# A two-layer backbone block on one core: layer 1's merge with tokens on the partitions, and one adaLN projection moved from TensorE to VectorE

## The chip, the core and the metric

The program runs on one core of one Trainium2 chip. The metric is the device time in microseconds of one execution. The engines are called as the profile calls them: PE is TensorE's matmul side and PEld its weight load, DVE is VectorE, ACT is ScalarE, POOL is GpSimd, SP is SyncE, which here issues the DMAs.

## The reference

Two layers over 256 latent tokens and 256 context tokens of 1024 channels. Each layer mixes tokens in three parallel branches (windowed attention A, global attention B, a bidirectional gated linear recurrence C), merges them with sigmoid gates, projects, and runs a squared-ReLU MLP. The shift, scale and gate rows of both halves come from adaLN projections of a conditioning vector. Layer 1 needs the latent stream alone in the merge, the output projection and the MLP.

```python
def _merge(ya, yb, yc, g, w_br_a, w_br_b, w_br_c, w_out):
    ga, gb, gc = jnp.split(jax.nn.sigmoid(g), N_BRANCH, axis=-1)
    return (ga * (ya @ w_br_a) + gb * (yb @ w_br_b) + gc * (yc @ w_br_c)) @ w_out
...
for l in range(DEPTH):
    with_ctx = l < DEPTH - 1
    mod_lat = (jax.nn.silu(c) @ w_ada[l] + b_ada[l])[:, None, :]
    mod_ctx = (jax.nn.silu(c_ctx) @ w_ada[l] + b_ada[l])[None, None, :]
    sh1, sc1, g1, sh2, sc2, g2 = jnp.split(mod_lat, 6, axis=-1)
    ...
    o_lat, o_ctx = _token_mixer(x * (1.0 + sc1) + sh1, ctx * (1.0 + csc1) + csh1, ...)
    x = _layernorm(ALPHA * x + g1 * o_lat, ln1_g[l], ln1_b[l])
    x = _layernorm(ALPHA * x + g2 * _sq_relu_mlp(x * (1.0 + sc2) + sh2, w_ff1[l], w_ff2[l]),
                   ln2_g[l], ln2_b[l])
```

## The kernel before

**Products.** Every float32 matrix is split into a rounded high part and the rest, and a product is three matmuls: high by high, high by rest, rest by high. The weights come in units of 1 MB (512 KB for the branch matrices of A and B), one DMA each into one of three `raw` buffers. ACT rounds a unit in four pieces into `whi` (`split`, L120), DVE subtracts for `wlo` (L128); in the recurrence stage every second piece of `whi` is DVE's too (L122). `take` hands out the next unit, and `prefetch` behind it issues the next loads and queues the next unit's pieces; `tick`, called between matmuls, emits them.

**Two forms of product.** `cm` keeps 128 channels of a weight unit stationary and moves the tokens: 512 columns in layer 0, 256 in layer 1, result with channels on the partitions (`ps_cm`). `tm` and `unit` keep 128 tokens stationary and move 256 or 512 weight columns, result with tokens on the partitions (`ps_tm`).

**Stages.** In each layer: recurrence (`lru`, with the key and value projections, and in layer 1 the first queries), attention interleaved by `pair` with a filler, which holds the other queries, the merge gates (`merge_gates`) and the branch products (`merge_branch`); then output projection (`wout`), residual, LayerNorm and transposes into channels (`tail_units`, `ln_t`, `ln_h`), MLP. In the span of the profiled execution layer 1's recurrence runs from about 940 to 1145 us, attention with the merge from 1100 to 1284, the output projection to 1306, the MLP to the end.

**Layer 1's merge.** The twelve gate units and the twelve branch units go through `cm` with 256 columns: 3 x 4 x 2 x 8 x 3 = 576 matmuls for the gates, 2 x 4 x 2 x 4 x 3 + 4 x 2 x 8 x 3 = 384 for the branches, 960 in all. ACT takes the tanh of each 128x256 gate block out of PSUM, DVE multiplies it with the branch block (L1163) and adds it up (L1168), and the sum's blocks, channels on the partitions, are split for the output projection.

**adaLN projections.** Beside the first one, each projection covers 2048 columns in eight steps of 128 rows. `ada_queue` plans them, `ada_step`, called from `prefetch`, starts the next step when the planner's PE time has passed `ada_at`: it first emits what is left of the step before, then the step's 1 MB load into a `raw` buffer. With `dve` set a step is eight DVE instructions that multiply and add 128x512 (L293, the first step L291), emitted one at a time by `tick` over the pace `ADA_PACE`, and PE adds the partitions up once at the end; without it a step is four 512-column matmuls on PE. The planner's time runs on its own costs (0.42 ns a column). While steps are queued, `prefetch` loads weights two units ahead, else three:

```python
self.emit_dma(i + 3 if not self.ada_q else i + 2)
```

**Order.** The framework orders each engine's instructions when the kernel is built; an engine then runs them strictly in that order, so a DVE instruction that waits holds back all DVE instructions behind it, and with them the `wlo` pieces that PE needs next.

Of the kernel before, what the change touches and what calls it, by code (L numbers as in the profile page):

```python
# [9 lines left out]
F32R = mybir.dt.float32r  # L10
AF = mybir.ActivationFunctionType
# [36 lines left out]
class Kern:  # L48
# [95 lines left out]
    def plan_units(self):  # L144
# [9 lines left out]
        for l in range(DEPTH):  # L154
            win = a["w_in"][l]
            order = ("xr0 yr0 xr1 yr1 xr2 yr2 xr3 yr3 kvA qA0 kvB qA1 qB0 qB1",
                     "xr0 xr1 yr0 yr1 kvA xr2 yr2 kvB xr3 yr3 qA0 qA1 qB0 qB1")[l]
            for n in order.split():
                key = (n,) if n[:2] == "kv" else (n[:2], int(n[2]))
                U.append(((l,) + key, cols(win, COL[key[0]] + 256 * sum(key[1:])), KD))  # L160
            for what, br in self.MERGE[l]:
                for n in range(4):
                    if what == "g":
                        U.append(((l, "g", br, n), cols(win, COL["g"] + 1024 * "abc".index(br) + 256 * n), KD))
                    else:
                        k = KD if br == "c" else KD // 2
                        U.append(((l, "br", br, n), cols(a["w_br_" + br][l], 256 * n, 0, k), k))
            for n in range(2):
                U += [((l, "wo", n, h), wide(a["w_out"][l], 512 * n, 512 * h), KD) for h in range(2)]
            f1 = [((l, "f1", n // 4, n % 4), cols(a["w_ff1"][l], 256 * n), KD) for n in range(16)]  # L170
            f2 = [((l, "f2", q, n, h), wide(a["w_ff2"][l], 512 * n, 1024 * q + 512 * h), KD)
                  for q in range(4) for n in range(2) for h in range(2)]
            for q in range(4):
                U += f1[4 * q + (q > 0):4 * q + 5] + f2[4 * q:4 * q + 4]
# [13 lines left out]
            self.u_dma += 1  # L188

    def is_wide(self, i):  # L190
        return self.units[i][0][1] in ("wo", "f2")

    def shaped(self, t, i):

# [128 lines left out]
            else:  # L323
                self.ada_q.append((lambda k=k: dma(k), [], lambda k=k: mms(k), 0.0))

    ADA_PACE = (9500, 18000)

    ADA = (('bra0',0,4,1),('bra0',0,8,1),('mlp0',1,0,1),('mlp0',1,4,1),('ga1',1,8,0))

    def ada_start(self, at):  # L330
        for a, l, b, dve in self.ADA:
# [792 lines left out]
    def merge_gates(self, l, br):  # L1124
# [1 line left out]
        cols = BOTH if l == 0 else LAT  # L1126
        self.tg[br] = []
        for n in range(4):
            w = self.take((l, "g", br, n))
            if br == "c":  # L1130
                if n == 1:
                    while any(step[2] for step in self.bg):
# [5 lines left out]
                elif n > 1:  # L1138
# [3 lines left out]
                        self.y["C"].append((hi, lo))  # L1142
                    if n == 3:
                        self.flags.add((l, "y", "C"))
            for b, t in enumerate(self.g2(l, "tg")):
                yield from self.cm(w, self.h, cols, b)
                self.act(t[:, cols], self.out, AF.Tanh, scale=0.5)
                self.tg[br].append(t)

    def merge_branch(self, l, br, first, last):  # L1150
        nc = self.nc
# [1 line left out]
        k = KD if br == "c" else KD // 2  # L1153
        while (l, "y", br.upper()) not in self.flags:
            yield "need"
        ys = self.y.pop(br.upper())
        for n in range(4):
            w = self.take((l, "br", br, n))
# [131 lines left out]
    def tail_units(self, l, which, keys, xs):  # L1290
# [6 lines left out]
            self.hn = [(self.g("h_hi", F32R), self.g("h_lo", F32R)) for _ in range(KD)]  # L1297
        if l:
            ws = []
            for tb, j in ((2, 0), (2, 1), (3, 0), (3, 1)):  # L1300
                if tb == 2:
                    ws.append(self.take(keys[j]))
                self.unit(keys[j], ws[j], xs, (tb,), True)
# [46 lines left out]
    def wout(self, l):  # L1350
        self.start_residual(l, 1)
        if l == 0:
            self.load_x(l)
        for h in range(2):
            self.unit((l, "wo", 0, h), self.take((l, "wo", 0, h)), self.m_hl(), self.tbs, True)
        self.tail_units(l, 1, [(l, "wo", 1, 0), (l, "wo", 1, 1)], self.m_hl())
        self.m = {}

# [112 lines left out]
    def layer(self, l):  # L1471
        a = self.a
        self.ada_start("layer%d" % l)
        self.layer_consts(l)
        self.ks, self.qs, self.qt, self.vv, self.y, self.m, self.tg, self.qs_at = {}, {}, {}, {}, {}, {}, {}, {}
        self.lru(l)
        if l == 0:
# [122 lines left out]
```

## Time and profile before

| | |
|---|---|
| median of three timed runs | 1508.69 us (1506.35 to 1509.06) |
| the profiled execution | 1507.38 us, its span 1505.6 us |
| busy, share of the span | PE 97%, PEld 81%, DVE 77%, ACT 51%, POOL 19% |
| mean granted TensorE clock | 0.989 |
| matmuls | 8364 records |

The page's shares are means over very different stages; the windows of the trace give them for a stretch, the chain of waits tells what ended last, and the timeline of an engine shows each instruction with the idle time before it and what ended that. A matmul's own duration overlaps its neighbours', so a matmul is priced by a row of many divided by their number, and a DVE instruction from its start to the next one's start.

### The profile page before, as it was taken

What the parts mean: (1) busy time and instruction counts of PE and PEld (TensorE: products, weight loads), DVE (VectorE), ACT (ScalarE), POOL (GpSimd) and SP (SyncE); (2) the same over time, 40 slices, a digit from 0 to 9 for tenths busy, and PEclk for the clock granted to TensorE, in tenths of its full rate; (3) what the DMA queues carried; (4) which work ended last, traced back from release to release, by engine and by line L of the source; (5) the groups of instructions that cost most, each with busy time, mean ns of one, the idle gap of its engine ahead of it and who ended that gap; (6) DMA issues with size and microseconds to landing.
All of it is one profiled execution on the core that took longest, in us unless ns stands there. A gap on an engine that the chain in (4) does not pass through costs nothing.

```text
span 1505.6 us, 22308 instructions
## 1 busy us (share of the span) xinstructions
PE 1455.2 (97%) x8364; PEld 1226.5 (81%) x8364; DVE 1154.4 (77%) x2179; ACT 772.2 (51%) x1594; POOL 292.7 (19%) x298
## 2 busy tenths in 40 slices
PE   7899999999999999899999999999899999899997
PEld 4688988777878879678878887897787899799986
DVE  4699987758688966977657768888989577886666
ACT  2698667565223327313323234587777655655452
POOL 0533422100000002711110301264411003031110
PEclk9999999999999999999999999999999999999999
DMA  9523310105557552444435343342345735755563
GB/s 325 194 85 111 113 57 29 43 29 172 169 190 247 198 198 95 159 160 159 162 112 192 116 168 110 107 143 74 123 144 178 243 109 185 251 169 186 181 193 112
DMA packets 156748, 225.69 MB, mean 150 GB/s; under 512 B 5840, under 2 KB 118992, under 8 KB 151520
## 3 DMA queue, kind: packets, MB, share of 16 engines
q1 hardware_dynamic: 156640, 224.27, 45.2%
q8 instruction: 65, 1.06, 0.3%
q14 instruction: 43, 0.35, 0.1%
HBM read 218.97 MB, written 5.28 MB: 149 GB/s over the span
## 4 chain that ended last, share of the span: by engine, by line
PE 80%; DVE 12%; ACT 4%; issue 2%; DMA 1%; POOL 0%; SPq 0%; DVEq 0%; ACTq 0%
PE ps_cm L92 42%; PE ps_tm L92 26%; DVE wlo L128 3%; PE ps_s L92 2%; PE ps_pv L92 2%; PE ps_pT L99 2%; PE ps_ada L92 2%; PE ps_gate L92 2%; DVE ada_acc L293 1%; DVE xc L647 1%; DMA raw_ada<-in_w_ada_dram 1%; PE ps_qT L99 1%; ACT L103 1%; DVE lru_q L718 1%; DVE lru_i L708 0%
## 5 line engine op out<-in xcount | busy, mean ns | idle before, releaser
L120 ACT CAST whi<-raw 128x512 fp32r<-128x512 f32 x521 | 300.1, 622 | 374.0 <-PE ps_tm L92 195.3
L128 DVE TENSOR_TENSOR wlo<-raw,whi 128x512 fp32r<-128x512 f32 x560 | 407.0, 753 | 103.2 <-ACT whi L120 98.0
L92 PE MATMUL ps_cm<-h_hi,wlo 128*128 128x256 f32 (+1 forms) x1216 | 406.9, 337 | 7.0 <-DVE wlo L128 6.9
L92 PE MATMUL ps_cm<-h_hi,whi 128*128 128x256 f32 (+1 forms) x1216 | 408.5, 340 | 3.0 <-ACT whi L120 2.0
L92 PE MATMUL ps_cm<-h_lo,whi 128*128 128x256 f32 (+1 forms) x1216 | 406.1, 336 | 0.2 <-POOL h_lo L1249 0.2
L92 PEld LDWEIGHTS ps_cm<-h_hi,whi 128*128 128x128 f32 x1216 | 230.4, 191 | 39.9 <-ACT whi L120 7.1
L92 PEld LDWEIGHTS ps_cm<-h_hi,wlo 128*128 128x128 f32 x1216 | 231.9, 191 | 34.3 <-DVE wlo L128 9.2
L92 PEld LDWEIGHTS ps_cm<-h_lo,whi 128*128 128x128 f32 x1216 | 232.0, 191 | 24.1 <-POOL h_lo L1249 0.7
L293 DVE SCALAR_TENSOR_TENSOR ada_acc<-raw_ada,silu,ada_acc 128x512 f32<-128x512 f32 x224 | 168.7, 799 | 49.6 <-DMA raw_ada<-in_w_ada_dram 49.4
L92 PE MATMUL ps_tm<-wlo,f_hi 128*128 128x512 f32 x384 | 150.2, 392 | 2.1 <-DVE wlo L128 2.1
L92 PE MATMUL ps_tm<-whi,f_hi 128*128 128x512 f32 x384 | 149.7, 390 | 0.0
L92 PE MATMUL ps_tm<-whi,f_lo 128*128 128x512 f32 x384 | 149.3, 389 | 0.0
L1188 POOL TENSOR_TENSOR x<-x,res 128x512 f32<-128x512 f32 x36 | 51.9, 1445 | 306.8 <-DVE res L1187 306.8
L92 PE MATMUL ps_tm<-wlo,h_hi 128*128 128x256 f32 x320 | 92.0, 287 | 6.1 <-DVE wlo L128 6.0
L92 PE MATMUL ps_tm<-whi,h_hi 128*128 128x256 f32 x320 | 92.9, 290 | 1.2 <-ACT lru_r L103 0.6
L92 PE MATMUL ps_tm<-whi,h_lo 128*128 128x256 f32 x320 | 91.4, 286 | 0.0
L92 PEld LDWEIGHTS ps_tm<-wlo,f_hi 128*128 128x128 f32 x384 | 72.1, 188 | 19.6 <-DVE wlo L128 5.2
L92 PEld LDWEIGHTS ps_tm<-whi,f_hi 128*128 128x128 f32 x384 | 72.1, 188 | 15.7 <-ACT whi L120 0.8
L103 ACT ACTIVATE p<-ps_s,mx 128x512 f32<-128x512 f32 (+1 forms) x96 | 58.5, 618 | 51.2 <-DVE mx L1001 29.9
L92 PEld LDWEIGHTS ps_tm<-whi,f_lo 128*128 128x128 f32 x384 | 72.1, 188 | 14.8
L685 POOL TENSOR_TENSOR lru_i<-lru_i,xc 128x512 f32<-128x512 f32 x32 | 52.8, 1680 | 89.3 <-ACT lru_i L103 89.3
L92 PEld LDWEIGHTS ps_tm<-wlo,h_hi 128*128 128x128 f32 x320 | 62.0, 194 | 7.7 <-DVE wlo L128 7.3
(173 smaller groups left out, 2449.5 us busy)
## 6 DMA issues: line engine op xcount, KB each, us to landing
raw<-in_w_ff_dram SPq DMA_DIRECT2D x64, 1024.0 KB, 5.5
raw<-in_w_in_dram SPq DMA_DIRECT2D x50, 1024.0 KB, 5.1
raw_ada<-in_w_ada_dram SPq DMA_DIRECT2D x40, 1024.0 KB, 5.0
w_ada<-in_w_ada_dram SPq DMA_DIRECT2D x32, 256.0 KB, 5.6
raw<-in_w_br_c_dram SPq DMA_DIRECT2D x8, 1024.0 KB, 5.7
raw<-in_w_out_dram SPq DMA_DIRECT2D x8, 1024.0 KB, 5.0
gw_raw<-in_v_gate_dram SPq DMA_DIRECT2D x16, 256.0 KB, 5.3
raw<-in_w_br_a_dram SPq DMA_DIRECT2D x8, 512.0 KB, 3.5
```

Of the source, the lines that this page charges most:

```text
L92: self.nc.tensor.matmul(out, lhsT, rhs, start=start, stop=stop, **kw)
L99: self.nc.tensor.transpose(out, in_, self.ident if n == 128 else self.ident[0:n, 0:n])
L103: ins = self.nc.scalar.activation(out, in_, func, **kw).ins
L120: self.nc.scalar.copy(out, in_)
L128: return self.nc.vector.tensor_tensor(lo, src, hi.bitcast(F32), op=ALU.subtract)
L293: self.nc.vector.scalar_tensor_tensor(acc, w, c, acc, op0=ALU.mult, op1=ALU.add)
L647: nc.vector.scalar_tensor_tensor(o, r3[:, :, lo_ + d:lo_ + d + n], w(j), o, op0=ALU.mult, op1=ALU.add)
L685: nc.gpsimd.tensor_tensor(ig, ig, self.xc[k[0]][0], op=ALU.mult)
L718: nc.vector.tensor_tensor_scan(h[:, cs][:, ::-1], r[:, cs][:, ::-1], ig[:, cs][:, ::-1], init, op0=ALU.mult, op1=ALU.add)
L1188: (nc.vector if last else nc.gpsimd).tensor_tensor(x, x, t, op=ALU.add)
```

## The change

Four edits.

1. **Weight units of layer 1's merge.** Gates and branches are loaded as 512 rows by 512 columns: four units for each gate (column half `n`, row half `h`), two each for branches A and B, four for C, so that every unit is 1 MB and one load.
2. **Tokens on the partitions.** `tw` computes them with 128 tokens stationary and 512 weight columns moving, for the two token blocks, over two units where the rows need two; two PSUM tiles stay open in between. It is 480 matmuls of 512 columns. Tanh, product and sum are taken at 128x512: 12, 12 and 8 instructions in place of 24, 24 and 16. `merge_t` transposes the sum back into channels on PE, 2 x 8 transposes of 128x128, and splits it; the first half stands inside the last branch unit, the second inside the first unit of the output projection, which for this is taken token block by token block.
3. **Order of the last two units of layer 1's output projection**: both token blocks on the first unit, then both on the second (before: both units on the first block, then on the second).
4. **The third projection of layer 1** (`sc2`, `g2`): from PE steps started at the first gate of layer 1 to DVE steps queued behind the two others at the start of layer 0's MLP; the pace of layer 1's projections goes from 18000 to 10500.

```diff
             for what, br in self.MERGE[l]:
+                if l:
+                    for n in range(2):
+                        for h in range(2 if what == "g" or br == "c" else 1):
+                            if what == "g":
+                                src = wide(win, COL["g"] + 1024 * "abc".index(br) + 512 * n, 512 * h)
+                            else:
+                                src = wide(a["w_br_" + br][l], 512 * n, 512 * h)
+                            U.append(((l, what, br, n, h), src, KD))
+                    continue
...
-    ADA_PACE = (9500, 18000)
+    ADA_PACE = (9500, 10500)
 
-    ADA = (('bra0',0,4,1),('bra0',0,8,1),('mlp0',1,0,1),('mlp0',1,4,1),('ga1',1,8,0))
+    ADA = (('bra0',0,4,1),('bra0',0,8,1),('mlp0',1,0,1),('mlp0',1,4,1),('mlp0',1,8,1))
...
+    def tw(self, w, xs, tb, h, n_h, po):
+        whi, wlo = w
+        if h == 0:
+            po[tb] = self.ps("ps_tw")
+        o, ts = po[tb], slice(128 * tb, 128 * tb + 128)
+        for i in range(4):
+            xhi, xlo = xs[4 * h + i]
+            self.mm(o, xhi[:, ts], whi[:, i, :], h == 0 and i == 0, False)
+            self.mm(o, xhi[:, ts], wlo[:, i, :], False, False)
+            self.mm(o, xlo[:, ts], whi[:, i, :], False, h == n_h - 1 and i == 3)
+            self.tick()
+            yield
...
+    def merge_t(self, n):
+        for j in range(2):
+            p = self.ps("ps_m")
+            for b in range(2):
+                for tb in range(2):
+                    c = 128 * (2 * j + b)
+                    self.tp(p[:, 256 * b + 128 * tb:256 * b + 128 * tb + 128], self.m[2 * n + tb][:, c:c + 128])
+            hi, lo = self.g("m_hl", F32R), self.g("m_hl", F32R)
+            self.split(hi, lo, p)
...
-            for tb, j in ((2, 0), (2, 1), (3, 0), (3, 1)):
+            for tb, j in ((2, 0), (2, 1), (3, 0), (3, 1)) if final else ((2, 0), (3, 0), (2, 1), (3, 1)):
```

**Where the projection's steps come to stand: SP's queue at the end of layer 0's MLP.** `raw_ada` is the load of one step, `raw` that of a weight unit (`w_ff` the MLP's, `w_in` those of layer 1's recurrence), `b_ada` the bias load that goes with the eighth step of a projection. Before:

```order
L276 DMA raw_ada<-in_w_ada_dram 128x2048
L186 DMA raw<-in_w_ff_dram 128x4x512 x2
L276 DMA raw_ada<-in_w_ada_dram 128x2048
L186 DMA raw<-in_w_in_dram 128x8x256 x2
L285 DMA b_ada<-in_b_ada_dram 32x512 x4
L186 DMA raw<-in_w_in_dram 128x8x256 x2
L406 DMA gd<-gate_rows 2x512 x2
L1270 DMA xd<-x 128x512 x4
L186 DMA raw<-in_w_in_dram 128x8x256
L628 DMA gw_raw<-in_v_gate_dram 128x512 x2
```

After:

```order
L287 DMA raw_ada<-in_w_ada_dram 128x2048
L196 DMA raw<-in_w_ff_dram 128x4x512 x2
L296 DMA b_ada<-in_b_ada_dram 32x512 x4
L287 DMA raw_ada<-in_w_ada_dram 128x2048
L196 DMA raw<-in_w_in_dram 128x8x256
L417 DMA gd<-gate_rows 2x512 x2
L287 DMA raw_ada<-in_w_ada_dram 128x2048
L196 DMA raw<-in_w_in_dram 128x8x256 x2
L287 DMA raw_ada<-in_w_ada_dram 128x2048
L196 DMA raw<-in_w_in_dram 128x8x256
L1344 DMA xd<-x 128x512 x4
L196 DMA raw<-in_w_in_dram 128x8x256
```

Before, the last step's load of the second projection stands directly ahead of the loads of layer 1's first units, and nothing of the third is there. After, the second projection ends one step earlier, and the third one's eight loads begin behind the last unit of layer 0's MLP and stand among the loads of layer 1's recurrence, the eighth 27 rows further on.

**What DVE then has in front of it: its order around the first scan of layer 1's recurrence.** `lru_q` and `lru_i` are the recurrence's, `wlo` the pieces of the units that PE takes next, `ada_acc` the projection. Before:

```order
L122 CAST whi<-raw 128x512
L128 TENSOR_TENSOR wlo<-raw,whi 128x512 x4
L122 CAST whi<-raw 128x512 x2
L700 SCALAR_TENSOR_TENSOR lru_q<-lru_q,lru_th 128x512
L128 TENSOR_TENSOR wlo<-raw,whi 128x512 x3
L700 SCALAR_TENSOR_TENSOR lru_q<-lru_q,lru_th 128x512 x3
L128 TENSOR_TENSOR wlo<-raw,whi 128x512
L708 TENSOR_TENSOR lru_i<-lru_i,lru_q 128x512 x4
L715 SCALAR_TENSOR_TENSOR lru_q<-lru_r,lru_i 128x512
```

After:

```order
L304 SCALAR_TENSOR_TENSOR ada_acc<-raw_ada,silu,ada_acc 128x512 x5
L128 TENSOR_TENSOR wlo<-raw,whi 128x512 x3
L304 SCALAR_TENSOR_TENSOR ada_acc<-raw_ada,silu,ada_acc 128x512
L128 TENSOR_TENSOR wlo<-raw,whi 128x512
L304 SCALAR_TENSOR_TENSOR ada_acc<-raw_ada,silu,ada_acc 128x512
L122 CAST whi<-raw 128x512 x2
L304 SCALAR_TENSOR_TENSOR ada_acc<-raw_ada,silu,ada_acc 128x512
L711 SCALAR_TENSOR_TENSOR lru_q<-lru_q,lru_th 128x512
L128 TENSOR_TENSOR wlo<-raw,whi 128x512 x3
L711 SCALAR_TENSOR_TENSOR lru_q<-lru_q,lru_th 128x512 x3
L128 TENSOR_TENSOR wlo<-raw,whi 128x512
L304 SCALAR_TENSOR_TENSOR ada_acc<-raw_ada,silu,ada_acc 128x512 x3
```

Eleven multiply-adds of the projection stand where there was none; five of them come ahead of the `wlo` pieces of the next unit. All 64 of the third projection are found on DVE between the residual of layer 0's last unit and the third batch of layer 1's recurrence: 16 ahead of layer 1, 8 before the first scaled tokens are split, 16 around the first batch, 16 around the second, 8 in the third.

**The end of layer 1's merge on PE.** `ps_cm` (before) and `ps_tw` (after) are the last branch's products, `ps_tm` the output projection, `ps_m` the new transposes. Before:

```order
L92 MATMUL ps_cm<-y_hl,wlo 128x256
L92 MATMUL ps_cm<-y_hl,whi 128x256 x2
L92 MATMUL ps_cm<-y_hl,wlo 128x256
L92 MATMUL ps_tm<-whi,m_hl 128x512
L92 MATMUL ps_tm<-wlo,m_hl 128x512
L92 MATMUL ps_tm<-whi,m_hl 128x512 x2
L92 MATMUL ps_tm<-wlo,m_hl 128x512
```

After:

```order
L92 MATMUL ps_tw<-whi,y_hl 128x512 x2
L92 MATMUL ps_tw<-wlo,y_hl 128x512
L92 MATMUL ps_tw<-whi,y_hl 128x512
L99 MATMUL ps_m<-ident,tg 128x128 x8
L92 MATMUL ps_tw<-whi,y_hl 128x512
L92 MATMUL ps_tw<-wlo,y_hl 128x512
L92 MATMUL ps_tw<-whi,y_hl 128x512 x2
```

The eight transposes of the first half stand between the two token blocks of the last branch unit; the other eight follow in the same way behind the first twelve matmuls of the output projection.

## Rows read from the trace of the kernel before

**Rows 1.** The page, part 1: busy time by engine, share of the span, instructions.

```profile
PE 1455.2 (97%) x8364; PEld 1226.5 (81%) x8364; DVE 1154.4 (77%) x2179; ACT 772.2 (51%) x1594; POOL 292.7 (19%) x298
```

**Rows 2.** Windows: length; PE, PEld, DVE, ACT, POOL busy (count); PEclk; DMA share; GB/s.

```profile
600.00:660.00 60.00, 55.60 (x239) 43.46 (x238) 54.25 (x65) 18.18 (x34) 27.39 (x17) 1.00 0.51 170
870.00:940.00 70.00, 70.00 (x325) 56.41 (x323) 48.79 (x84) 27.09 (x53) 6.44 (x8) 1.00 0.39 130
...
966.00:1000.00 34.00, 32.41 (x241) 30.84 (x241) 30.32 (x53) 28.88 (x55) 12.05 (x9) 1.00 0.42 140
1050.00:1100.00 50.00, 41.93 (x276) 37.56 (x275) 45.98 (x77) 34.54 (x63) 21.43 (x27) 0.97 0.36 116
1150.00:1200.00 50.00, 50.00 (x401) 41.76 (x401) 34.00 (x77) 32.10 (x76) 6.88 (x9) 1.00 0.75 246
1260.00:1284.00 24.00, 24.00 (x202) 24.00 (x202) 14.74 (x33) 12.16 (x27) 2.46 (x2) 1.00 0.50 156
```

**Rows 3.** Chain that ended last, whole span: start us, us, what.

```profile
929.22 1.26 PE ps_z L99 x8
...
1391.13 21.79 PE ps_tm L92 x96
1412.91 23.03 PE ps_cm L92 x192
```

**Rows 4.** Timeline of PE: start us, us, engine line op tiles, count [idle before].

```profile
759.58 1.92 PE L92 MATMUL ps_ada<-ada_acc,pick 128*32 128x512 f32 x16
761.44 0.50 PE L92 MATMUL ps_tm<-whi,f_hi 128*128 128x512 f32 x1
...
1115.38 1.07 PE L92 MATMUL ps_ada<-raw_ada,silu 128*32 128x512 f32 x8
1116.37 0.39 PE L92 MATMUL ps_cm<-h_hi,whi 128*128 128x256 f32 x1
```

**Rows 5.** Timeline of DVE, layer 0's MLP, columns as in rows 4.

```profile
604.74 6.52 DVE L293 SCALAR_TENSOR_TENSOR ada_acc<-raw_ada,silu,ada_acc 128x512 f32<-128x512 f32 x5
611.18 1.51 DVE L122 CAST f_hi<-relu 128x512 fp32r<-128x512 f32 x1
...
634.31 2.73 DVE L293 SCALAR_TENSOR_TENSOR ada_acc<-raw_ada,silu,ada_acc 128x512 f32<-128x512 f32 x4
636.96 0.68 DVE L128 TENSOR_TENSOR wlo<-raw,whi 128x512 fp32r<-128x512 f32 x1
```

**Rows 6.** Windows of the six stretches that receive projection steps, columns as rows 2.

```profile
921.00:941.00 20.00, 20.00 (x105) 14.99 (x104) 13.95 (x28) 10.69 (x23) 6.44 (x8) 1.00 0.27 87
949.00:957.00 8.00, 7.81 (x61) 7.13 (x60) 4.91 (x12) 4.17 (x10) 0.73 (x1) 1.00 0.86 298
970.00:1020.00 50.00, 49.90 (x328) 45.88 (x329) 44.95 (x75) 38.49 (x71) 26.70 (x23) 1.00 0.40 132
1020.00:1036.00 16.00, 15.03 (x114) 14.03 (x113) 11.55 (x18) 10.93 (x20) 3.00 (x4) 1.00 0.21 67
1036.00:1062.00 26.00, 23.11 (x117) 18.78 (x115) 24.86 (x38) 17.05 (x31) 16.62 (x19) 0.93 0.35 112
1066.00:1093.00 27.00, 21.79 (x151) 19.48 (x150) 24.25 (x39) 26.90 (x48) 6.12 (x4) 1.00 0.38 126
```

**Rows 7.** Timeline of PE, start of layer 1: four first matmuls after a wait.

```profile
970.10 0.39 PE L92 MATMUL ps_cm<-h_hi,wlo 128*128 128x256 f32 x1 [1.59 <-DVE wlo L128]
...
1067.43 0.39 PE L92 MATMUL ps_tm<-wlo,h_hi 128*128 128x256 f32 x1 [1.42 <-DVE wlo L128]
...
1093.66 0.42 PE L92 MATMUL ps_tm<-wlo,h_hi 128*128 128x256 f32 x1 [2.77 <-DVE wlo L128]
...
1140.85 0.39 PE L92 MATMUL ps_cm<-h_hi,wlo 128*128 128x256 f32 x1 [1.93 <-DVE wlo L128]
```

**Rows 8.** Tile ada_acc, 560 to 1000 us: DVE idle before it, us, times.

```profile
  DMA raw_ada<-in_w_ada_dram: 37.0, 12
```

**Rows 9.** Timeline of PE behind layer 1's output projection, columns as rows 4.

```profile
1311.11 1.47 PE L99 MATMUL ps_z<-ident,x 128*128 128x128 f32 x8 [3.86 <-DVE x L1226]
```


## Prediction before the run

> **What bounds the kernel now.** I read the shares first: PE is busy for 97% of the span, DVE for 77% [rows 1]. A mean over unlike stages cannot say what a moved instruction costs, so I went to the windows [rows 2]. PE is full in the last stretch of layer 0's MLP (870 to 940: 70.00 of 70 us) and in layer 1's attention and merge (1150 to 1200 and 1260 to 1284, every microsecond); DVE is idle there for a third of the time. There the time is the sum of PE's work. The start of layer 1 is another matter: of 50 us from 1050 PE works 41.93, DVE 45.98, ACT 34.54, and from 966 to 1000 DVE has 30.32 of 34. The timeline of PE shows who is waited for there: at four places along the recurrence and the start of the attention PE stands idle 1.42 to 2.77 us for a `wlo` piece, which DVE makes [rows 7]. In that stage a microsecond put on DVE ahead of a `wlo` piece is paid by PE, apart from what DVE's idle time takes in.
>
> **PE's part of the change: about -9.8 us, in the stage where PE is full.**
>
> *Wider matmuls.* The chain has runs of both forms without a gap: 192 matmuls of `ps_cm` in 23.03 us are 119.9 ns each, 96 of `ps_tm` in 21.79 us are 227.0 [rows 3]. Two matmuls of 256 columns are thus 239.9 ns, one of 512 is 227.0, and 480 pairs save 480 x 12.9 ns = 6.2 us. The runs are other stages' matmuls in the same two forms; the merge's weight load has kept PEld busy for the whole of 1260 to 1284 [rows 2], which is the kind of stretch that gains from half the loads.
>
> The Trainium skill (TensorE: Matmul & The Clock Gate, section "Back-to-back issue gap") gives the isolated spacing of a warm matmul as columns / 2.4 plus 2.5 ns, so a pair would save only the 2.5 ns, 1.2 us in all, and the total would be 5 us higher. The rows differ from it (120 and 227 against 109 and 216 ns) and decide.
>
> *Transposes.* `merge_t` adds 16 transposes of 128x128. Eight `ps_z` in a row take 1.26 us in the chain [rows 3], 0.157 each: +2.5.
>
> *The third projection.* One of its PE steps runs from 1115.38 to 1116.37, 0.99 us to the next matmul [rows 4]. Eight of them go: -7.9. The final sum over the partitions comes in: the one at 759.58 takes 1.86 until the next matmul [rows 4]. Net -6.1. Together -6.2 + 2.5 - 6.1 = -9.8.
>
> **DVE's part: +22.3 us, in the stage where DVE is nearly full.** The third projection becomes 64 multiply-adds. By name they belong to layer 0's MLP, but a step starts only where a unit of weights starts and the planned pace has run out. An MLP unit is 48 matmuls of 512 columns, by the planner's 0.42 ns a column 10,322 ns; the new pace, 10,500, is just more, so a step still comes with every second unit, as with 18,000. The MLP has room for the two earlier projections only, and the orders above show all 64 adds from the residual of its last unit to the third batch of the recurrence.
>
> Price of one: alone, four adds take 636.96 - 634.31 = 2.65 us, 0.66 each; beside POOL, five take 611.18 - 604.74 = 6.44 us, 1.29 each [rows 5]. These two are the bounds. POOL is busy for 59.6 us of the 147 in the six receiving stretches (6.44 + 0.73 + 26.70 + 3.00 + 16.62 + 6.12), 41% [rows 6], which by mixing would give 0.66 + 0.41 x 0.63 = 0.92. But POOL's work is a fixed amount, and DVE was busy beside nearly all of it already (124.5 of the 147 us): what it slows is in the rows of before, and an add put there mostly moves another DVE instruction out of POOL's way. So I take 0.70, near the lower row.
>
> What hides them is DVE's idle time in the stretch in which they are written [rows 6]:
>
> - 921 to 941: 16 adds, 11.2 us, idle 20 - 13.95 = 6.05: +5.1
> - 949 to 957: 8 adds, 5.6, idle 3.09: +2.5
> - 970 to 1020: 16 adds, 11.2, idle 5.05: +6.1
> - 1020 to 1036: 8 adds, 5.6, idle 4.45: +1.1
> - 1036 to 1062: 8 adds, 5.6, idle 1.14: +4.5
> - 1066 to 1093: 8 adds, 5.6, idle 2.75: +2.8
>
> That is 44.8 us of adds against 22.5 of idle time, +22.3 (the terms rounded). I pass it to the end in full, since behind each stretch stands one of PE's waits for `wlo` [rows 7], so that a late DVE is not caught up unseen. Bounds: if idle time between these stretches takes in what the adds leave, and PE's work ahead of a stretch covers the first 5.1, about +12; if every second add meets POOL at 1.29, the price is 0.97, the sum 64 x 0.97 - 22.5 = +39.6; with only every fourth, 0.82, it is +30.
>
> **What I cost at nothing or nearly.** The earlier two projections in the MLP keep their pace; PE's slack (55.60 of 60 us even from 600 to 660, where POOL is beside DVE, 27.39 us of it [rows 2]) decides little there, and that the second step now follows the first directly I take as 0, between -2 and +4. DVE waited for `raw_ada` loads 12 times in the MLP, 37.0 us, 3.1 each [rows 8]; PE is full behind that (870 to 940) and hides it, but in the recurrence such a wait would hold back `wlo` pieces. As the loads are issued at a unit's start and the next step's adds come a unit later, I take 0, up to +10; the same bound holds for the weights that are now fetched two units ahead, not three, and share three `raw` buffers with these loads. The merge's 12, 12 and 8 wider instructions are fewer on DVE, which has 9.26 us of 24 free by 1284 [rows 2]: 0. Two open PSUM tiles over two units, while the attention also wants tiles: 0, up to +4. The order of the output projection's last two units lets the first block's residual start later than before; PE waited 3.86 us for `x` there [rows 9], and the last twelve matmuls of 227 ns cover 2.7 us of one block's residual: +0.5, between -1 and +2.
>
> **The sum.** -9.8 + 22.3 + 0.5 = +13.0. The profiled execution took 1507.4 us (the span of 1505.6 and 1.8 around it), which makes 1520.4; it lies 1.3 below the median of 1508.7, so on the medians 1521.7, predicted as **1522**.
>
> **The rivals.**
>
> *The adds are hidden.* From 870 to 940 DVE carries such adds at no cost to PE, which is full [rows 2]. If the adds slide into places where PE has work in hand, only -9.3 is left: about 1499. For it: from 970 to 1020 PE works 49.90 of 50 us although DVE is at 90% [rows 6], so its `wlo` pieces mostly come in time, and the wait is short. Against it: 44.8 us of work does not go into 22.5 of idle time, and DVE runs in order. It decides from whether the waits of [rows 7] grow by more than a microsecond or two each. 0.18.
>
> *Half hidden.* The price is 0.66 and the spaces between the stretches absorb about half of the surplus: +10 against -9.3, within 0.2% of the median (1505.7 to 1511.7; 0.2% is about what a measurement of this kernel can tell from no change). 0.12.
>
> *POOL's lock.* The recurrence keeps POOL busy, 26.70 us of the 50 from 970 [rows 6]; if the 40 adds from 970 on pay 1.29 in place of 0.70 [rows 5], that is 40 x 0.59 = +23.6, and the time is about 1545. Against it: POOL's work there is limited and ends. The Trainium skill (SBUF — State Buffer, section "Who interferes with whom") says that a DVE instruction with two inputs in SBUF contends with a GpSimd instruction that reads it; the add has two, and the row of 1.29 agrees. 0.08.
>
> *The projection is where its name says.* If all eight steps were in layer 0's MLP, DVE's idle time there (21.21 us in the 70 from 870 [rows 2]) would help hide them, and the result is the first rival's, 1499. The orders exclude it; nothing is added.
>
> **How the numbers follow.** My forecast, DVE pays for most of the adds, has 0.62 and its own range is 1512 to 1536: from the +12 bound to +30 with a few microseconds of the open terms that are nought in the sum. Hidden 0.18, half hidden 0.12, POOL's lock 0.08. Hence faster 0.18, same 0.12, slower 0.70. The range that should hold the time 8 times in 10 leaves out the lock and most of the hidden case: 1502 to 1537.
>
> **What would show it.** In the profile after, PE's time between 1100's counterpart and the end of the merge is shorter by about 10 us, the `ps_tw` matmuls cost 227 ns, and the `ps_ada` steps are gone from it. Layer 0's MLP ends when it did. From the last unit of that MLP to the end of the recurrence the program takes about 22 us longer, DVE is above 95% busy there, the adds cost about 0.70 us, and the waits for `wlo` at the counterparts of [rows 7] are longer or more. Wrong would be: the recurrence as long as before (then the adds were hidden), adds of over 1 us (POOL), DVE waiting on `raw_ada` in the recurrence (the load, not the adds), or merge matmuls at 240 ns a pair's worth (no gain on PE).

## The result, and the profile after

| | before | after |
|---|---|---|
| median of the timed runs | 1508.49 us (4 runs, 1506.35 to 1509.06) | 1528.83 us (4 runs, 1527.96 to 1529.47) |
| ratio to before | | 1.0136, 95% interval 1.0125 to 1.0148 |
| span of the profiled execution | 1505.6 us | 1527.1 us |
| mean granted TensorE clock | 0.989 | 0.979 |

The change costs 20.3 us. The forecast was 1522, in a range of 1502 to 1537. The sign, the stage that pays and the mechanism came out as the prediction had them. One large term, PE's gain, did not; DVE's term was too high, which hid part of that.

The first lines of the page of the kernel after, busy time by engine with the share of the span (compare [rows 1]): PE does 512 matmuls less and is busy 4.7 us more, DVE 42.1 us more.

```profile
PE 1459.9 (96%) x7852; PEld 1208.7 (79%) x7852; DVE 1196.5 (78%) x2219; ACT 770.5 (50%) x1578; POOL 298.3 (20%) x298
```

Where the time went is read from windows cut at events that both kernels have: the first transpose (`ps_z`) behind layer 0's MLP, the last one, the first attention scores (`ps_s`) of layer 1, the last `ps_z` behind layer 1's output projection. The five stretches are the MLP of layer 0, its tail, the recurrence, the attention with merge and output projection, and the rest. Columns: length; PE, PEld, DVE, ACT and POOL busy (with instructions); granted clock; DMA share; GB/s. First the kernel before:

```profile
584.40:925.40 341.00, 336.60 (x1547) 277.11 (x1547) 246.91 (x387) 107.30 (x204) 64.55 (x44) 1.00 0.45 150
925.40:949.70 24.30, 23.71 (x150) 18.93 (x149) 19.16 (x40) 11.42 (x25) 8.48 (x9) 1.00 0.19 66
949.70:1100.30 150.60, 137.15 (x905) 123.88 (x905) 129.68 (x215) 111.22 (x206) 65.67 (x66) 0.98 0.34 112
1100.30:1312.60 212.30, 206.24 (x1534) 181.14 (x1533) 166.81 (x383) 135.93 (x303) 21.58 (x21) 0.99 0.57 185
1312.60:1505.60 193.00, 183.14 (x1152) 166.95 (x1152) 135.82 (x228) 94.32 (x201) 33.84 (x24) 0.97 0.54 172
```

The same stretches of the kernel after:

```profile
585.00:927.00 342.00, 338.64 (x1566) 279.60 (x1565) 249.21 (x394) 107.75 (x205) 68.99 (x45) 1.00 0.46 150
927.00:956.00 29.00, 24.61 (x145) 21.31 (x143) 28.98 (x59) 12.42 (x27) 8.72 (x8) 0.94 0.53 182
956.00:1122.80 166.80, 145.13 (x913) 128.76 (x912) 160.79 (x263) 111.09 (x205) 68.66 (x68) 0.93 0.39 131
1122.80:1334.50 211.70, 200.30 (x1005) 155.13 (x1004) 165.13 (x351) 132.97 (x286) 20.06 (x20) 0.97 0.46 151
1334.50:1527.00 192.50, 181.34 (x1153) 164.56 (x1152) 136.35 (x228) 94.63 (x201) 33.81 (x24) 0.99 0.51 165
```

The MLP is 1.0 us longer, the tail 4.7, the recurrence 16.2; in these two DVE is now busy for 189.8 of 195.8 us. The attention with the merge is only 0.6 us shorter, although PE has fewer and wider matmuls there, and the rest is as before. So the recurrence pays, and the stage with the merge gives next to nothing back.

One place shows the mechanism, at its most expensive. It is DVE's timeline of the kernel after (start, us, instruction, count), then POOL's and PE's at the same time, with the idle time ahead in brackets:

```profile
983.25 7.92 DVE L304 SCALAR_TENSOR_TENSOR ada_acc<-raw_ada,silu,ada_acc 128x512 f32<-128x512 f32 x5
991.09 4.46 DVE L128 TENSOR_TENSOR wlo<-raw,whi 128x512 fp32r<-128x512 f32 x3
```

```profile
983.12 6.48 POOL L696 TENSOR_TENSOR lru_i<-lru_i,xc 128x512 f32<-128x512 f32 x4 [11.11 <-ACT lru_i L103]
```

```profile
990.40 0.28 PE L92 MATMUL ps_cm<-h_hi,wlo 128*128 128x256 f32 x1
990.52 0.28 PE L92 MATMUL ps_tm<-whi,h_hi 128*128 128x256 f32 x1
993.91 0.58 PE L92 MATMUL ps_tm<-wlo,h_hi 128*128 128x256 f32 x1 [3.11 <-DVE wlo L128]
...
994.50 0.41 PE L92 MATMUL ps_tm<-whi,h_hi 128*128 128x256 f32 x1
994.71 0.41 PE L92 MATMUL ps_tm<-wlo,h_hi 128*128 128x256 f32 x1
994.92 0.41 PE L92 MATMUL ps_tm<-whi,h_lo 128*128 128x256 f32 x1
```

Five adds stand ahead of the `wlo` pieces, as the order said. They meet POOL's product of the recurrence and take 7.84 us to the next start, 1.57 each; this is more than most adds take, the median of the 56 of steps two to eight is 0.74. The pieces behind them come late, and PE, which had a matmul every 0.12 us, stands idle for 3.11 us. Then it goes on with one every 0.21 us: the granted clock has fallen to the lower of its two levels (1.2 GHz), 0.92 on the mean from 956 to 1000 us. An add ahead of a `wlo` piece thus costs DVE its own time, and PE a pause and, here, slower matmuls behind it.

### The profile page after: what moved, and what is told of

The parts are those of the page before. It is cut to its first block, busy times and chain, and to the rows that moved or that the text cites. A ratio compares the mean times of both kernels' runs of the same rounds, so it can differ in the third digit from the quotient of the medians.

```text
span 1527.1 us, 21279 instructions
## 1 busy us (share of the span) xinstructions
PE 1459.9 (96%) x7852; PEld 1208.7 (79%) x7852; DVE 1196.5 (78%) x2219; ACT 770.5 (50%) x1578; POOL 298.3 (20%) x298
## 4 chain that ended last, share of the span: by engine, by line
PE 73%; DVE 17%; issue 6%; ACT 3%; DMA 1%; POOL 0%; SPq 0%; DVEq 0%; ACTq 0%; POOLq 0%
PE ps_cm L92 35%; PE ps_tm L92 23%; PE ps_tw L92 5%; DVE wlo L128 4%; DVE ada_acc L304 3%; PE ps_pv L92 2%; PE ps_s L92 2%; PE ps_pT L99 2%; PE ps_ada L92 2%; DVE xc L658 1%; PE ps_gate L92 1%; DVE lru_q L729 1%; DMA raw_ada<-in_w_ada_dram 1%; ACT L103 1%; DVE p L1027 1%
## 5 line engine op out<-in xcount | busy, mean ns | idle before, releaser
L92 PE MATMUL ps_cm<-h_hi,wlo 128*128 128x512 f32 (+1 forms) x1024 | 351.7, 346 | 4.4 <-DVE wlo L128 4.4
L92 PE MATMUL ps_cm<-h_hi,whi 128*128 128x512 f32 (+1 forms) x1024 | 351.4, 348 | 3.1 <-ACT whi L120 2.0
L92 PE MATMUL ps_cm<-h_lo,whi 128*128 128x512 f32 (+1 forms) x1024 | 351.9, 346 | 1.7 <-POOL h_lo L1323 0.8
L304 DVE SCALAR_TENSOR_TENSOR ada_acc<-raw_ada,silu,ada_acc 128x512 f32<-128x512 f32 x280 | 217.0, 817 | 46.0 <-DMA raw_ada<-in_w_ada_dram 45.9
L92 PEld LDWEIGHTS ps_cm<-h_hi,wlo 128*128 128x128 f32 x1024 | 194.5, 190 | 30.4 <-DVE wlo L128 5.7
L92 PEld LDWEIGHTS ps_cm<-h_hi,whi 128*128 128x128 f32 x1024 | 193.5, 191 | 30.8 <-ACT whi L120 3.8
L92 PEld LDWEIGHTS ps_cm<-h_lo,whi 128*128 128x128 f32 x1024 | 194.9, 191 | 26.1 <-POOL h_lo L1323 2.3
L1262 POOL TENSOR_TENSOR x<-x,res 128x512 f32<-128x512 f32 x36 | 55.4, 1545 | 299.6 <-DVE res L1261 299.6
L103 ACT ACTIVATE p<-ps_s,mx 128x512 f32<-128x512 f32 (+1 forms) x96 | 58.4, 615 | 55.1 <-DVE mx L1012 37.6
L414 POOL TENSOR_SCALAR gate_rows<-ada_rows 128x512 f32<-128x512 f32 x4 | 7.0, 1740 | 320.7 <-DVE ada_rows L316 266.4
```

Source lines behind the costliest of these rows:

```text
L92: self.nc.tensor.matmul(out, lhsT, rhs, start=start, stop=stop, **kw)
L103: ins = self.nc.scalar.activation(out, in_, func, **kw).ins
L304: self.nc.vector.scalar_tensor_tensor(acc, w, c, acc, op0=ALU.mult, op1=ALU.add)
L414: self.nc.gpsimd.tensor_scalar(t, rows, (0.5, 1.0)[which] / ALPHA, None, op0=ALU.mult)
L1262: (nc.vector if last else nc.gpsimd).tensor_tensor(x, x, t, op=ALU.add)
```

## The experiments

Times are medians with the ratio to the kernel before, which was measured beside them on the same chip, and its 95% interval.

| kernel | us | ratio |
|---|---|---|
| merge alone | 1505.91 | 0.9986 (0.9976 to 0.9995) |
| projection alone | 1531.13 | 1.0153 (1.0138 to 1.0168) |
| after, without 56 of the 64 adds | 1505.52 | 0.9981 (0.9971 to 0.9990) |
| after, 28 of the 56 adds | 1514.27 | 1.0040 (1.0025 to 1.0055) |
| after, those 56 adds made twice | 1566.39 | 1.0379 (1.0362 to 1.0396) |
| merge alone, two of eight PE steps | 1502.12 | 0.9960 (0.9945 to 0.9975) |
| merge alone, old order behind it | 1505.63 | 0.9984 (0.9974 to 0.9993) |
| after, pace 9500 | 1519.51 | 1.0078 (1.0063 to 1.0093) |
| the same, late sums | 1507.75 | 0.9998 (0.9989 to 1.0008) |
| late sums, even pace | 1511.35 | 1.0022 (1.0012 to 1.0032) |
| late sums, slow start | 1505.57 | 0.9989 (0.9979 to 0.9998) |

### Which half of the change costs: each one alone

The merge alone is the changed kernel with the old plan of projections:

```diff
-    ADA_PACE = (9500, 10500)
+    ADA_PACE = (9500, 18000)
-    ADA = (..., ('mlp0',1,8,1))
+    ADA = (..., ('ga1',1,8,0))
```

> The changed kernel with its third projection as before (eight PE steps in layer 1's merge, pace 18000); the merge with tokens on the partitions and the new order stay. Theory A (the merge saves what was summed, 6.2 us for the wider matmuls less 2.5 for the transposes, and what the whole change lost in the attention came from DVE being late out of the recurrence): the recurrence is as before and the time is 3 us under before, about 1505. Theory B (the merge itself brings new waits into the attention, because its filler steps are twice as long and two PSUM tiles stay open): the saving is given back there, the time is 1508 to 1513, and PE waits for p as in the changed kernel.

The projection alone is the kernel before with the plan of the changed one:

```diff
-    ADA_PACE = (9500, 18000)
+    ADA_PACE = (9500, 10500)
-    ADA = (..., ('ga1',1,8,0))
+    ADA = (..., ('mlp0',1,8,1))
```

> The kernel before with the third projection's queue and pace of the changed one alone; merge and order as before. Theory A (DVE's adds cost the recurrence what the trace of the changed kernel shows, 22.5 us up to the first attention scores, and DVE's lateness costs more behind that): 22.5 less the eight PE steps of 0.99 us that are gone, plus some 8 of waits and clock in the attention: 1528 to 1532. Theory B (the attention's loss belongs to the merge): 22.5 - 7.9 = +14.6, about 1523.

Measured: -2.3 us for the merge alone against the kernel before that was measured beside it, and +22.9 for the projection alone. The two add up to 20.6, the change itself makes 20.3, so they do not depend on each other much. Theory A's times hold in both. The merge saves 2.3 us where 3.2 were summed for it; its interval, 0.8 to 3.6 us, holds both. The projection costs more than the prediction's +22.3 - 6.1 = +16.2, because the attention of that kernel, 211.6 us from the first scores to the last `ps_z`, is as long as before (212.3), though eight PE steps are gone from it. PE's timeline of the projection alone shows the largest of the pauses that fill their place:

```profile
1132.18 0.73 PE L92 MATMUL ps_s<-kT,qT 128*128 128x512 f32 x2 [1.98 <-ACT p L103]
...
1163.88 0.38 PE L92 MATMUL ps_cm<-h_hi,wlo 128*128 128x256 f32 x1 [2.49 <-DVE wlo L128]
...
1190.75 0.63 PE L99 MATMUL ps_qT<-ident,qstk 128*128 128x128 f32 x4 [2.41 <-ACT kT L120]
```

### Is it DVE's time, or the loads: the adds left out, halved, doubled

Without the adds, with the loads, the first step and the sums in place:

```diff
         def add(k, j, s):
+            if l and blocks[0] == 8 and k:
+                return
```

> The changed kernel without the 56 multiply-adds of the third projection's steps two to eight (so its sc2 and g2 come from the first step alone); loads, the first step and the final sums stay. Theory A (DVE's time is what the recurrence pays for): some 56 x 0.7 = 39 us of DVE less, recurrence within 4 us of before, 1499 to 1508. Rival (the loads take raw buffers and weights are fetched one unit less ahead): the recurrence stays 15 us or more longer than before and the time is 1520 or more.

Half of them, and twice as many:

```diff
         def add(k, j, s):
+            if l and blocks[0] == 8 and k and s:
+                return
```

> The changed kernel with half of the third projection's adds in steps two to eight (only those of the first of its two rows of conditioning, 28 of 56, so the other row's sc2 and g2 are incomplete). Theory A (the sum of the prediction: DVE's idle time in a stretch takes in adds until it is full, only what goes over it is paid): with half the adds only about 3 us are over, the first attention scores start within 4 us of the kernel without these adds (1102.3 us), the total is 1504 to 1511. Rival (DVE's idle time is not to be had, because it waits there for ACT and for PE in a chain of which the adds become a part: every add costs its share from the first): half of the 20.5 us between that kernel and the changed one, first scores at about 1112, the total about 1517.

```diff
-                self.nc.vector.scalar_tensor_tensor(acc, w, c, acc, op0=ALU.mult, op1=ALU.add)
+                for _ in range(2 if l and blocks[0] == 8 else 1):
+                    self.nc.vector.scalar_tensor_tensor(acc, w, c, acc, op0=ALU.mult, op1=ALU.add)
```

> The changed kernel with every add of the third projection in steps two to eight made twice (56 adds more, sc2 and g2 too large). Theory A (DVE's idle time is used up by the first 64): each further add is paid in full, 56 x 0.70 to 0.75 = 39 to 42 us more, about 1569. Rival (the price is the same share of an add from the first, 20.5 us for 56): 1549.

Measured: 1505.5 without the adds, so the loads, the shorter prefetch and the shared `raw` buffers cost little, and the adds are the cause. In the changed kernel, where the adds hold those buffers longer, DVE waits for a `raw_ada` load once in this stage, for 0.8 us. The first 28 adds cost 8.8 us (0.31 each), the next 28 14.6 (0.52 each), the 56 more 37.6 (0.67 each). Neither theory was quite right for the half: it lies 3 us above the one (1504 to 1511) and 3 below the other (1517). For the double, the 1566.4 are near the 1569 of theory A and far from 1549. The windows of the recurrence, from the last `ps_z` of layer 0 to the first scores, tell why; the rows are the kernels without, with half, with all and with twice the adds, columns as above:

```profile
950.70:1102.30 151.60, 138.41 (x912) 124.12 (x911) 130.41 (x222) 111.76 (x207) 66.00 (x68) 0.97 0.45 147
```

```profile
955.10:1110.90 155.80, 140.57 (x916) 126.50 (x915) 143.66 (x241) 111.40 (x205) 68.01 (x68) 0.94 0.43 141
```

```profile
955.80:1122.90 167.10, 145.43 (x915) 129.06 (x915) 161.09 (x265) 111.19 (x205) 68.69 (x68) 0.93 0.39 131
```

```profile
959.10:1164.50 205.40, 155.86 (x918) 135.25 (x917) 201.28 (x326) 114.02 (x206) 77.26 (x68) 0.88 0.36 118
```

DVE's idle time, the length less its busy time, is 21.2, 12.1, 6.0 and 4.1 us: it takes in adds, but less and less of each. Without the adds 17.7 of the 21.2 us are waits for ACT, 5.2 of them for `lru_q` and 4.7 for `h_hi`; with all of them 3.1 are left. That the adds lengthen the chain in which DVE waits there is a likely reason for their price, but no run tests it. And PE's busy time for the same matmuls grows from 138 to 156 us, as the clock falls from 0.97 to 0.88.

### Why the attention stage gave nothing back: PE steps left out of it

```diff
         def mms(k):
             if k == 0:
                 st["ps"] = self.ps("ps_ada")
+            if 0 < k < KD - 1:
+                return
```

> The kernel with the merge alone (third projection as PE steps beside the attention), of whose eight PE steps the second to the seventh leave out their matmuls (sc2 and g2 incomplete); loads and order otherwise the same. Six steps of 0.99 us are gone from PE and nothing comes to DVE. Theory A (PE is full there, as the prediction put it): 5.9 us less, about 1500. Theory B (the first steps stand in the first 60 us of the attention, where PE waits for ACT and DVE anyway, and cover such waits): at most 3 us less, 1503 to 1506.

Measured: 3.8 us less than the merge alone for six steps, 0.63 each, where the prediction had 0.99. Against the merge with the old order below, which was measured beside it, it is 3.5 us. Runs of one kernel lie up to 4 us apart, so that the saving is known to some 1.5 us: it is less than theory A's 5.9, and theory B's 3 is not excluded. Some of the steps did cover waits. PE's wait at the counterpart of 1140.85 [rows 7] shows it, first in the kernel with the merge alone, then with the six steps left out:

```profile
1140.07 0.50 PE L92 MATMUL ps_tw<-wlo,h_hi 128*128 128x512 f32 x1 [1.55 <-DVE wlo L128]
```

```profile
1139.30 0.80 PE L92 MATMUL ps_tw<-wlo,h_hi 128*128 128x512 f32 x1 [3.01 <-DVE wlo L128]
```

The prediction had taken PE as full in the whole attention, from a row that begins at 1150 [rows 2]. In the kernel before the first four of the eight steps stand at 1115 to 1151 us, where PE waits now and then for DVE, as at 1140.85 [rows 7].

The order of the output projection's last units, put back in the kernel with the merge alone:

```diff
-            for tb, j in ((2, 0), (2, 1), (3, 0), (3, 1)) if final else ((2, 0), (3, 0), (2, 1), (3, 1)):
+            for tb, j in ((2, 0), (2, 1), (3, 0), (3, 1)):
```

> The kernel with the merge alone, with the order of the last two units of layer 1's output projection as before (both units on one token block, then on the other). Theory A (the prediction's term of +0.5, between -1 and +2, for the new order): within 1.5 us of the kernel with the merge alone, 1504 to 1507; PE's wait for x behind the output projection goes from two waits of 2.71 and 0.59 us back to one of about 3.9. Rival (the new order costs or gains more, since both token blocks' residuals end late): beyond 2 us.

Measured: 1505.6 against 1505.9; the order makes no difference that can be measured. In the changed kernel PE's wait there is 2.71 us, where it was 3.86 [rows 9], but all sixteen transposes come behind it.

### Is there room in layer 0's MLP: other paces, later sums

```diff
-    ADA_PACE = (9500, 10500)
+    ADA_PACE = (9500, 9500)
```

> The changed kernel with layer 1's pace at 9500 in place of 10500. By the order a step then starts with every MLP unit, not every second, and all three projections lie in layer 0's MLP. Theory A (the 64 adds cost 22 us only because they stand in the recurrence): DVE has room in the MLP (it was busy about 70 per cent from 640 to 935 us), the recurrence is as before, PE's saving is left: 1508.5 - 9.3 = about 1499, or 1504 if the attention gives half back. Rival (the MLP has not the room, or the steps then wait for their loads on DVE, two steps' loads in the time of one): the MLP is 5 to 20 us longer and the time 1508 to 1520.

Measured: 1519.5, the rival. The recurrence is as before, but the MLP is 22.6 us longer. PE's timeline of this kernel shows its three longest pauses in that MLP: one for `wlo`, and two at the final sums, which the plan writes directly behind the last adds:

```profile
639.64 0.55 PE L92 MATMUL ps_tm<-wlo,f_hi 128*128 128x512 f32 x1 [3.88 <-DVE wlo L128]
...
694.29 3.39 PE L92 MATMUL ps_ada<-ada_acc,pick 128*32 128x512 f32 x10 [4.29 <-DVE ada_acc L304]
879.66 1.08 PE L92 MATMUL ps_ada<-ada_acc,pick 128*32 128x512 f32 x4 [3.23 <-DVE ada_acc L304]
```

So the sums were moved one weight unit on, which also leaves that unit without a new step:

```diff
+        if self.ada_pend is not None and not self.ada_late and self.units[self.u_cur][0][1] in ("f1", "f2"):
+            self.ada_late = True
+            self.ada_at = self.pe + 1000
+            return
+        self.ada_late = False
         if self.ada_pend is not None:
             self.ada_pend()
```

> The kernel with all three projections in layer 0's MLP (pace 9500, 1519.5 us), with each final sum over the partitions written one weight unit later, so that PE does not meet it while DVE still has the last step's adds in front of it (there PE waited 4.29 and 3.23 us for ada_acc). Theory A (the MLP has the room, and the sums' waits and the lower clock behind them make about half of its 22.6 us): 1508 to 1512. Rival (DVE is simply too full in the MLP, late pieces of wlo take over from the sums): 1515 to 1520.

Measured: 1507.7, 11.8 us less, 0.3 us below theory A's range and far from the rival's. The two pauses at the sums, 7.5 us together, are gone. The windows of its MLP and of its attention with merge and output projection:

```profile
584.40:935.70 351.30, 343.87 (x1587) 279.72 (x1587) 300.10 (x469) 107.54 (x204) 73.23 (x46) 1.00 0.51 170
...
1110.30:1312.00 201.70, 193.64 (x1002) 152.21 (x1001) 162.39 (x344) 133.57 (x287) 20.01 (x20) 0.99 0.48 159
```

The MLP is still 10.3 us longer than before. But the attention with the merge is 10.6 us shorter, which is what the prediction had for it: the PE work saved there is real, PE is busy 193.6 us in place of 206.2. In the changed kernel it is 200.3 busy, at a clock of 0.97 and not 0.99, and idle for 11.4 us in place of 8.1.

Two more plans for the same steps, with late sums: all 24 evenly spread, and only the first three at half the rate.

```diff
-    ADA_PACE = (9500, 9500)
+    ADA_PACE = (9500, 13000)
-            self.ada_at = self.pe + 1000
-            self.ada_at, ... = self.pe + pace, ...
+            self.ada_at, ... = max(self.ada_at + pace, self.pe) if pace == 13000 else self.pe + pace, ...
```

> The same with late sums, and the 24 steps spread evenly over the MLP (a step every 13000 ns of planned time on the average, so one or two units apart, the last one still inside the MLP) in place of one with every unit. Theory A (in the MLP 64 more adds fit into DVE's 88 us of idle time if they do not come in one dense run): MLP at most 8 us longer than before, the recurrence as before, the attention and merge about 8 us shorter as with pace 9500: 1502 to 1510, about even with the kernel with the merge alone. Rival (each add costs PE something wherever it stands): no better than 1512.

```diff
-    ... self.ADA_PACE[l]))
+    ... 10500 if l and blocks[0] == 0 and k < 3 else self.ADA_PACE[l]))
```

> The kernel with all three projections in layer 0's MLP and late sums (1507.8 us), whose first three steps, which run beside POOL's work at the start of the MLP, come with every second weight unit as in the kernel before; the others with every unit. Theory A (of the 10 us that the MLP is longer there, the waits for wlo of 3.93, 1.41, 0.71 and 0.58 us up to 690 us and the lower clock behind them come from the dense start beside POOL): 3 to 5 us less, 1503 to 1505. Rival (the surplus moves to the end of the MLP, where the last steps now stand): 1507 to 1510.

Measured: 1511.4 for the even pace, between the theories, and its interval reaches both: its MLP is 2.8 us longer again than with a step for every unit (354.1 against 351.3). But the adds do not cost it that wherever they stand. One pause of PE makes most of the 13.1 us by which this MLP is longer than before; at the same place the kernel before has waits of 2.24 and 1.36 us. These are PE's, DVE's and POOL's timelines there, then the window of the MLP's rest:

```profile
636.53 0.80 PE L92 MATMUL ps_cm<-h_hi,wlo 128*128 128x512 f32 x1 [12.20 <-DVE wlo L128]
```

```profile
618.17 10.23 DVE L304 SCALAR_TENSOR_TENSOR ada_acc<-raw_ada,silu,ada_acc 128x512 f32<-128x512 f32 x6
```

```profile
611.15 26.45 POOL L1346 TENSOR_TENSOR x<-x,ln_row 128x512 f32<-128x512 f32 x16 [18.42 <-DVE wlo L128]
```

```profile
640.00:939.50 299.50, 297.96 (x1327) 242.83 (x1327) 249.54 (x393) 87.00 (x159) 43.63 (x25) 1.00 0.53 175
```

Six adds stand ahead of the `wlo` pieces beside POOL's sixteen products and take 10.15 us to the next start, 1.69 each. From 640 us on PE is idle for 1.5 us of 299.5. So the MLP does have room for evenly spread adds, but not beside POOL's work at its start; an even pace that keeps clear of that was not tried. The slow start gives 1505.6, 2.2 us less than late sums at a constant pace (the intervals overlap), a smaller gain than the 3 to 5 us of theory A. It, the merge alone and the merge with the old order are the best complete versions found, each about 0.1% faster than the kernel before; which of the three is best these runs cannot tell.

## Why the prediction was right, and where its steps were off

**The stage and the cause: right.** The 64 adds stand in the recurrence and not in the MLP they are named for, DVE cannot take them in, and PE waits for `wlo`. The adds left out give 1505.5, and the same adds in the MLP leave the recurrence as it was.

**DVE's term, +22.3: near, a little high.** From the first `ps_z` behind the MLP to the first scores the kernel takes 195.8 us where it took 174.9. That is 20.9 more, and the sum over the partitions, which the prediction counted with PE, is in it with 1.9: 24.2 were forecast for the two. The 56 adds alone are 23.3 us over the whole span, some of it in the attention. The sum by stretches was too sharp: idle time is not free until it is full, as the halved adds show. The price of an add was about right. DVE's rows of `ada_acc` alone, from 915 to 1105 us, are 52.02 us for 64 instructions, 0.81 each with the overlap of their ends; eight of them are the first step's products, 0.48 us at the median (length; PE, PEld and DVE busy; clock, DMA, GB/s):

```profile
915.00:1105.00 190.00, 2.78 (x28) 0.55 (x20) 52.02 (x64) 0.94 0.41 138
```

**PE's term, -9.8: wrong as a gain of this kernel.** The step that failed is "in the stage where PE is full". The attention stage came out 0.6 us shorter, and with the sum apart the prediction had some 11 for it. So 10.5 us of gain did not come, DVE's term with the sum came 3.3 us cheaper than forecast, and the rest is small: the forecast was 7 us low, and without the second error it would have been 10 us low. As work the term is right, since late sums in the MLP give 10.6. Two things kept it from showing. The start of that stage is no place where PE is full, so six PE steps were worth some 3.8 us and not 5.9. And with the adds ahead of it PE is slower in the stage. PE's timeline of the kernel after has these pauses, of which the first two lie in the stage's first 40 us:

```profile
1130.91 0.73 PE L92 MATMUL ps_s<-kT,qT 128*128 128x512 f32 x2 [1.97 <-ACT p L103]
...
1159.10 1.21 PE L92 MATMUL ps_pv<-pT,v 128*64 128x256 f32 x8 [2.88 <-ACT p L103]
...
1272.44 0.87 PE L99 MATMUL ps_pT<-ident,p 128*128 128x128 f32 x2 [2.60 <-DVE p L1027]
1330.99 3.55 PE L99 MATMUL ps_z<-ident,x 128*128 128x128 f32 x16 [2.71 <-DVE x L1300]
```

The kernel without the 56 adds has the last three too. Its PE timeline, and its window from the first scores to the last `ps_z`:

```profile
1135.63 1.51 PE L92 MATMUL ps_pv<-pT,v 128*64 128x256 f32 x10 [3.02 <-ACT p L103]
...
1247.45 0.72 PE L99 MATMUL ps_pT<-ident,p 128*128 128x128 f32 x2 [2.63 <-DVE p L1029]
1304.59 3.76 PE L99 MATMUL ps_z<-ident,x 128*128 128x128 f32 x16 [2.71 <-DVE x L1302]
```

```profile
1102.30:1308.40 206.10, 195.86 (x1006) 153.06 (x1004) 164.92 (x351) 132.97 (x287) 20.01 (x20) 0.99 0.47 156
```

So with the adds the stage is 5.6 us longer (211.7 against 206.1), though none stands in it. Of this 4.4 us are PE's busy time for the same matmuls (200.3 against 195.9), at a granted clock of 0.97 in place of 0.99, and 1.2 are idle time.

**The parts of PE's term.** A wide matmul costs what was said: in a run of `ps_tw` three start in 0.68 us, 227 ns each. Of the rule that was weighed in the prediction and that its page gives for an isolated matmul (the Trainium skill, TensorE: Matmul & The Clock Gate, section "Back-to-back issue gap") the runs show no sign: by it the merge alone could not have saved anything, 1.2 us less the transposes, and it saved 2.3. The transposes were priced too high, at 0.157 from the tail of another stage; eight in the merge take 1302.63 - 1301.84 = 0.79 us, 0.10 each, so 16 are 1.6 us and not 2.5:

```profile
1298.21 0.62 PE L92 MATMUL ps_tw<-whi,y_hl 128*128 128x512 f32 x2
1298.66 0.39 PE L92 MATMUL ps_tw<-wlo,y_hl 128*128 128x512 f32 x1
1298.89 0.62 PE L92 MATMUL ps_tw<-whi,y_hl 128*128 128x512 f32 x2
...
1301.84 1.04 PE L99 MATMUL ps_m<-ident,tg 128*128 128x128 f32 x8
1302.63 0.48 PE L92 MATMUL ps_tw<-whi,y_hl 128*128 128x512 f32 x1
```

**The rivals.** Hidden adds did not come, nor half hidden ones. POOL's lock is real where it strikes, 1.57 us an add at 983 us, and the Trainium skill's rule (SBUF — State Buffer, section "Who interferes with whom") agrees with that row. In the changed kernel it strikes few adds; with the even pace, at 618 us, it made the longest pause. The last rival, that all steps in the MLP would be hidden and give 1499, was too simple: with pace 9500 it was 1519.5, and with late sums 1507.7. What the prediction did not name at all is the granted clock, which went from 0.98 to 0.93 in the recurrence, as behind the pause at 993.91. How much of that stage's length this costs is not shown: DVE, busy for 189.8 of 195.8 us from the tail to the first scores, may hold PE up there in any case.

**What stays open.** Why the granted clock in the attention stage is lower with the adds than without them is not shown. Behind the pause at 1272 us, far from any add, it fell to the lower level (first row), and behind the same pause in the kernel without the adds it did not (second row):

```profile
1272.40:1282.00 9.60, 9.56 (x47) 6.56 (x47) 4.81 (x10) 6.53 (x15) 0.00 (x0) 0.82 0.42 144
```

```profile
1247.40:1257.00 9.60, 9.48 (x55) 6.99 (x56) 6.07 (x11) 7.47 (x16) 0.00 (x0) 1.00 0.43 144
```

Nor is it shown why, with no adds at all, the stage is 206.1 us, when late sums give 201.7.

## What to carry to other kernels

Read an engine's room where the order puts the instructions, not where their name says, and ask stage by stage whether the engine that is relieved is full just there: six of the eight PE steps were worth about two thirds of their own time in a stage whose start alternates between engines. Idle time of an engine that sits in a chain is no free room: the first adds cost less than half their time, the last nearly all of it. Look for what runs beside the moved work: six adds beside POOL's products made one pause of 12.20 us. And a result that one in-order engine needs from another should be asked for one unit after it was queued; in layer 0's MLP, dense with adds, that was worth 11.8 us.

## What the runs showed of the hardware

A wait on PE can be paid twice. After a pause of 3.11 us the next 256-column matmuls started every 0.21 us in place of 0.12. Not every pause did this: behind one of 3.02 us, at 1135.63 in the kernel without the 56 adds, the granted clock stayed at 1.00:

```profile
1135.60:1145.00 9.40, 9.37 (x42) 5.87 (x43) 9.40 (x25) 8.30 (x22) 0.00 (x0) 1.00 0.38 123
```

In the four kernels with 0, 28, 56 and 112 adds the same matmuls of the recurrence kept PE busy 138.4, 140.6, 145.4 and 155.9 us, as the granted clock fell from 0.97 through 0.94 and 0.93 to 0.88. Beside POOL's products the same add took 1.57 and 1.69 us on DVE, where the median is 0.74.
